# A decoder layer in float32 on one core: the small second block's high and low parts side by side in TensorE's columns, a gather's transposes moved, and the startup's weight chunks shared between two engines

## The chip, the cores and the metric

One NeuronCore of a Trainium2 chip runs the kernel. The time is the device time of one execution in microseconds (us); a kernel's time is the median of its runs. Engines are named as the profile names them: PE is TensorE (PEld its weight loads), DVE is VectorE, ACT is ScalarE, POOL is GpSimd, SP is SyncE, whose queue issues most DMAs.

## The reference

One layer of a hybrid decoder on 1024 tokens of width 1024, in float32. `c` is the conditioning vector; `w_ada` turns it into shifts, scales and gates.

```python
mod = silu(c) @ w_ada + b_ada
shift_m, scale_m, gate_m, shift_f, scale_f, gate_f = split(mod, 6)
h = rms_norm(x, norm_mix) * (1 + scale_m) + shift_m
proj = h @ w_in                                   # 1024 x 8208
...
x = x + gate_m * (sum(gates * branch_proj) @ w_out)
h = rms_norm(x, norm_ffn) * (1 + scale_f) + shift_f
y = hier_moe(h, w_group, b_group, w_router, b_router, w_gate, w_up, w_down)
x = x + gate_f * y
```

The part left out holds three causal mixers (SSD, stick-breaking attention, gated DeltaNet). `hier_moe` picks one of four groups of experts for a token and two of its eight experts; an expert e computes

```python
(silu(xi @ w_gate[e]) * (xi @ w_up[e])) @ w_down[e]      # 1024 -> 512 -> 1024
```

## The kernel before

**Products.** A float32 product is made of three in the format fp32r: each operand is split into a high part (a copy rounded to fp32r, by ACT) and a low part (the difference, by DVE or POOL), in `split` (L296). `mm3` (L301) adds high by high, high by low and low by high in one PSUM tile. The left operand is the stationary one: its columns are the output's rows, and 512 columns of the right one stream past it.

**Order.** The kernel is emitted by streams (Python generators) with priorities. `Order` (L41) keeps a clock for each engine, adds up guessed costs in `note` (L72), and `run` (L170) lets the stream go next whose data is ready, the lower priority number first; a filler stream (projections, later the experts) takes the rest of PE's time. What it decides stands fixed in each engine's instruction list; every engine works its list in order. Nearly all instructions carry line 217, that of the helper that records them, so the rows are told apart by the names of tiles.

**Startup** (`startup`, L329). Eight tiles of 128 tokens, x0 to x7 (`x_sb`, four buffers), are loaded, normed (ACT sums the squares, `rsqrt` makes twelve small DVE operations, ACT and DVE scale) and transposed by PE into `xT`; half 0 is x0 to x3, half 1 x4 to x7. In parallel `gains` computes shift and scale: w_ada's first two blocks of columns come in 16 chunks `wa` of 0.5 MB (five buffers, reloaded by `loads`), four to each of four column groups c. For c = 0 and 1 PE multiplies both halves of each chunk with c (a 1-column stationary operand, `acc_row`); for c = 2 and 3 DVE does (`acc`), and PE transposes and DVE reduces at the end. Then `modulate(half)` makes the high and low parts `hT` of the modulated tokens from `xT`, row block kt by row block kt, and `weights` splits the first columns of w_in, job 0 and 1 (`w_raw`, `w_hi`, `w_lo`; job 1 is asked for ahead of wa12). `first` (L623) makes the first six output tiles of the projections (units) from whatever row block and weights are ready, 6 times 8 times 3 products, the 48 of one more pair of tiles are made by `cols`; the next job begins with products of 264 columns.

**Experts** (`moe`, L2294, filler; `moe_tokens` and `moe_hidden`, streams). The 32 experts come in a fixed order of places; each has one block of up to 128 tokens, and the one at place 12 (`TWICE`) a second block of 64 rows (`SECOND`), unit `u = NE`. For a block, `moe_tokens` gathers token rows into `e_xg` (two buffers, an indirect DMA on POOL's queue), PE transposes them into `e_pt`, and ACT and DVE split them into `e_xh` and `e_xl`. Weights come in pieces G, U and D of two halves of 1 MB (`e_raw`); ACT and DVE split each half in two parts (`e_hi`, `e_lo`, four buffers). Gate and up products (`e_pG`, `e_pU`) are 24 each, down products (`e_pd`) 24 on the split hidden values (`e_hh`, `e_hl`), which `hidden_parts` makes; `moe_finish` scales the result by the layer's gate and adds it to the output. For the second block each weight part is used a second time at once, 72 products more, in 64 of PE's 128 columns. The second expert's transposes (n = 1 in `moe_tokens`) are asked for 4000 planner's nanoseconds after their gather.

Of the kernel before, what the change touches and what calls it, by code (L numbers as in the profile page):

```python
# [19 lines left out]
P = 128  # L20
# [20 lines left out]
class Order:  # L41
# [30 lines left out]
    def note(self, eng, method, args, kw):  # L72
# [21 lines left out]
        else:  # L94
# [7 lines left out]
            elif eng == "DVE":  # L102
                fast = method in ("tensor_scalar", "tensor_copy", "memset")
# [132 lines left out]
class Trunk:  # L236
# [92 lines left out]
    def startup(self):  # L329
# [40 lines left out]
        sums = [ps.tile([P, W], F32, name=f"acc_row{c}", tag="pj", bufs=4)[0:1] for c in range(2)]  # L370
# [31 lines left out]
        def tokens():  # L402
            for half in range(2):
                tts = range(4 * half, 4 * half + 4)
                for tt in tts:
                    yield (xs[tt],)
# [13 lines left out]
                yield tuple(xs[tt] for tt in tts)  # L420
                for kt in range(KT):
                    pt = ps.tile([P, W], F32, name=f"xT_ps{half}_{kt}", tag="ps_t", bufs=2)
                    for q in range(4):
                        self.pe.transpose(pt[:, q * P:(q + 1) * P], xs[4 * half + q][:, kt * P:(kt + 1) * P], self.ident)
                    a.activation(xT[half][:, kt], pt, AF.Copy)
                    self.done.add(f"xT{half}_{kt}")
                    yield ()
                if half == 0:
                    columns(rows[1], 32)
                    for tt in range(4, 8):  # L430
                        load_x(tt)
                    self.done.add("x_in")

        def loads():
            for n in range(5, 16):
                yield from self.wait(f"acc{n - 5}")
                if n == 12:
                    yield from self.wait("w_split0", "x_in")
                    self.job_load(1)
                load_wa()  # L440

        def gains():

            yield from self.wait("col")
            for c in range(4):
                acc = sp.tile([P, 2, 256], F32, name=f"acc{c}", tag="acc", bufs=2)
                for q in range(4):
# [13 lines left out]
                if c < 2:  # L461
                    row = acc[0:1].rearrange("p m n -> p (m n)")
                    a.activation(row, sums[c], AF.Copy)
                    yield (row,)
                    red = ps.tile([P, W], F32, name=f"acc_ps{c}", tag="ps_t", bufs=2)[:, 0:4]
                    for j in range(4):
                        self.pe.matmul(red[:, j:j + 1], row[:, j * P:(j + 1) * P], self.ones[0:1, 0:1], start=True, stop=True)
                else:
                    yield (acc,)
                    pt = ps.tile([P, W], F32, name=f"acc_ps{c}", tag="ps_t", bufs=2)  # L470
                    for j in range(4):
                        self.pe.transpose(pt[:, j * P:(j + 1) * P], acc[:, j // 2, (j % 2) * P:(j % 2 + 1) * P], self.ident)
                    red = sp.tile([P, 4], F32, name=f"red{c}", tag="red", bufs=2)
                    v.tensor_reduce(red, pt.rearrange("p (a b) -> p a b", b=P), AX.X, ALU.add)
# [6 lines left out]
        def modulate(half):  # L481
            sl = slice(half * W, (half + 1) * W)
            for kt in range(KT):
# [2146 lines left out]
```

## Time and profile before

| | us |
|---|---|
| median of 3 runs | 1964.72 |
| lowest, highest | 1963.37, 1967.28 |
| the profiled execution | 1962.96 |
| its span in the profile | 1961.2 |
| busy: PE, DVE, ACT, POOL | 1865.1, 1352.5, 1107.4, 553.0 |

The span runs from the first to the last instruction of the profiled execution. A busy time is the sum over an engine's instructions; PE and PEld overlap. The mean granted clock of PE was 0.979 of full speed. The largest groups of instructions are the splits of the experts' weights (`e_hi` 407.4 us on ACT, `e_lo` 456.5 us on DVE) and the projections' products (453.8 us for the high parts of 1408 products alone).

### The profile page before, as it was taken

To read this page: it belongs to the slowest core of one execution; us is meant where nothing else is said; L and a number is where in the kernel's file an instruction comes from. 1 tells how busy PE (TensorE), PEld (TensorE's weight loads), DVE (VectorE), ACT (ScalarE), POOL (GpSimd) and SP (SyncE) were. 2 spreads that over 40 slices of the span, in tenths; PEclk is the share of its full clock that TensorE was granted. 3 is DMA by queue.
4 is the path that set the end of the run, shared out by engine and by line. 5 is a ranking of instruction groups with operands and counts; after the bars stand their busy time and mean duration, and the time that the engine had idled before them with its cause. 6 is when DMAs were issued, how large, how long until landed. Compare 5 with 4: busy or idle time off the path is not lost. (4 is left out here: it accounts for less than half of the span.)

```text
span 1961.2 us, 29540 instructions
## 1 busy us (share of the span) xinstructions
PE 1865.1 (95%) x10069; PEld 1480.4 (75%) x10069; DVE 1352.5 (69%) x2329; ACT 1107.4 (56%) x1951; POOL 553.0 (28%) x1045
## 2 busy tenths in 40 slices
PE   5999999999999999999999998987999999999997
PEld 2797787799999988777788897875777776665553
DVE  3546776647746334666425666676999979999996
ACT  6525666632224356776534435425777857888775
POOL 2300357542426441100001034101111124444322
PEclk9999999999999999999999999987999999999999
DMA  9363666788688764432447656676999999999994
GB/s 286 81 156 102 171 181 204 217 226 226 166 193 265 179 173 119 102 92 61 87 159 218 204 166 199 237 263 239 357 350 364 364 341 329 356 324 366 378 370 128
DMA packets 331491, 441.20 MB, mean 225 GB/s; under 512 B 53686, under 2 KB 200384, under 8 KB 331338
## 3 DMA queue, kind: packets, MB, share of 16 engines
q1 hardware_dynamic: 323898, 418.80, 67.8%
q0 software_dynamic: 7296, 20.42, 4.7%
q8 instruction: 80, 1.31, 0.3%
q14 instruction: 73, 0.60, 0.1%
q10 hardware_dynamic: 144, 0.07, 0.0%
HBM read 365.15 MB, written 77.71 MB: 226 GB/s over the span
## 5 line engine op out<-in xcount | busy, mean ns | idle before, releaser
L217 ACT ACTIVATE e_hi<-e_raw 128x1024 fp32r<-128x1024 f32 (+1 forms) x386 | 407.4, 1057 | 138.0 <-PE e_pU L217 58.4
L217 DVE TENSOR_TENSOR e_lo<-e_raw,e_hi 128x1024 fp32r<-128x1024 f32 (+1 forms) x386 | 456.5, 1212 | 38.4 <-ACT e_hi L217 34.5
L217 PE MATMUL pj<-hT,w_hi 128*128 128x512 f32 x1408 | 453.8, 403 | 3.2 <-DVE m_b L217 1.3
L217 PEld LDWEIGHTS pj<-hT,w_hi 128*128 128x128 f32 x1408 | 259.5, 189 | 65.1 <-issue 8.8
L217 PE MATMUL pj<-hT,w_lo 128*128 128x512 f32 x704 | 276.6, 393 | 0.0
L217 PE MATMUL pj<-w_hi,hT 128*128 128x256 f32 (+1 forms) x1280 | 257.1, 292 | 2.1 <-ACT cv L217 0.9
L217 PEld LDWEIGHTS pj<-w_hi,hT 128*128 128x128 f32 x1280 | 207.0, 192 | 5.2 <-issue 1.7
L217 PE MATMUL pj<-w_lo,hT 128*128 128x256 f32 (+1 forms) x640 | 181.8, 284 | 0.0
L217 POOL DMA_INDIRECT out_dram<-e_y,p_row x33 | 123.9, 3756 | 182.2 <-DVE e_y L217 131.2
L217 PEld LDWEIGHTS pj<-hT,w_lo 128*128 128x128 f32 x704 | 133.0, 189 | 29.0
L217 DVE SCALAR_TENSOR_TENSOR cv<-pre,col,cv 128x512 f32<-128x512 f32 x120 | 99.7, 831 | 77.8 <-ACT cv L217 75.0
L217 DVE TENSOR_TENSOR w_lo<-w_raw,w_hi 128x512 fp32r<-128x512 f32 (+1 forms) x116 | 83.7, 721 | 96.4 <-ACT w_hi L217 93.3
L217 POOL DMA_INDIRECT e_xg<-h2D,e_idx x33 | 64.0, 1941 | 266.4 <-PE e_pt L217 242.1
L217 PEld LDWEIGHTS pj<-w_lo,hT 128*128 128x128 f32 x640 | 123.0, 192 | 0.6
L217 PE MATMUL e_pU<-e_lo,e_xh 128*128 128x512 f32 (+9 forms) x264 | 104.3, 395 | 3.7 <-DVE e_lo L217 3.7
L217 PE MATMUL e_pG<-e_hi,e_xh 128*128 128x512 f32 (+9 forms) x264 | 107.3, 406 | 0.0
L217 PE MATMUL e_pG<-e_hi,e_xl 128*128 128x512 f32 (+9 forms) x264 | 104.4, 396 | 0.0
L217 PE MATMUL e_pG<-e_lo,e_xh 128*128 128x512 f32 (+9 forms) x264 | 104.4, 395 | 0.0
L217 PE MATMUL e_pU<-e_hi,e_xh 128*128 128x512 f32 (+9 forms) x264 | 104.2, 395 | 0.0
L217 PE MATMUL e_pU<-e_hi,e_xl 128*128 128x512 f32 (+9 forms) x264 | 103.7, 393 | 0.0
L217 PE MATMUL e_pd<-e_hi,e_hh 128*128 128x512 f32 (+9 forms) x248 | 101.7, 410 | 0.0
L217 POOL TENSOR_TENSOR t_lo<-t_raw,t_hi 128x512 fp32r<-128x512 f32 x16 | 21.3, 1329 | 283.6 <-ACT t_hi L217 174.3
(470 smaller groups left out, 4006.7 us busy)
## 6 DMA issues: line engine op xcount, KB each, us to landing
e_raw<-in_w_gate_dram SPq DMA_DIRECT2D x64, 1024.0 KB
e_raw<-in_w_up_dram SPq DMA_DIRECT2D x64, 1024.0 KB
e_raw<-in_w_down_dram SPq DMA_DIRECT2D x63, 1024.0 KB
w_raw<-in_w_in_dram SPq DMA_DIRECT2D x124, 256.0 KB
m_wa<-in_w_ada_dram SPq DMA_DIRECT2D x64, 256.0 KB
brD<-br SPq DMA_DIRECT2D x48, 256.0 KB
t_raw<-in_w_branch_dram SPq DMA_DIRECT2D x16, 768.0 KB
t_gate<-brD SPq DMA_DIRECT2D x16, 768.0 KB
```

The source lines that it names most:

```text
L217: return f(*a, **k)
```

## The change

It has three parts, and one line of the planner's costs.

1. **The second block.** For unit `NE`, the high and the low part of its 64 rows lie side by side in one tile of 128 stationary columns, tokens and hidden values alike. `mm_block` makes two products where `mm3` made three: the pair with the weights' high part (output rows 0 to 63 high by high, rows 64 to 127 low by high), and the high part with the weights' low part, into rows 0 to 63. `two_parts` adds the two halves of the output: ACT copies rows 64 to 127 to rows 0 to 63 of an SBUF tile, DVE adds the others. It is used four times: gate, up, and the two halves of down.
2. **The second expert's transposes** wait for a flag "G0", set when the first expert's gate products have been emitted, in place of the 4000 ns.
3. **The startup.** Of each chunk of w_ada, PE takes one half (k = 0) and DVE the other; a column group is reduced by eight small products with a column of ones. Half 1's row blocks are modulated straight from PSUM, without the copy to `xT`, when their gain is there (`modulate(kt, half, x)`; `waiting` takes the others). x4 to x7 are loaded after wa12, job 1's weights after the last chunk; units 4 and 5 of `first` wait for the last gain; the streams have other priorities.

The planner's cost of a DVE copy or scaling is no longer the fast one where it reads PSUM.

```diff
@@ startup: tokens, loads
-                    a.activation(xT[half][:, kt], pt, AF.Copy)
-                    self.done.add(f"xT{half}_{kt}")
+                    if f"gam{kt // 2}" in self.done:
+                        modulate(kt, half, pt)
+                    else:
+                        a.activation(xT[half][:, kt], pt, AF.Copy)
+                        self.done.add(f"xT{half}_{kt}")
...
                 if half == 0:
                     columns(rows[1], 32)
-                    for tt in range(4, 8):
-                        load_x(tt)
-                    self.done.add("x_in")
+                    self.done.add("xT0")
...
-                if n == 12:
-                    yield from self.wait("w_split0", "x_in")
-                    self.job_load(1)
+                if n == 13:
+                    yield from self.wait("xT0")
+                    for tt in range(4, 8):
+                        load_x(tt)
                 load_wa()
+            yield from self.wait("w_split0")
+            self.job_load(1)
@@ startup: gains
-                    for k in range(2):
-                        kt = 2 * q + k
-                        if c < 2:
-                            self.pe.matmul(sums[c], cc[kt], was[n][:, k].rearrange("p m n -> p (m n)"), start=kt == 0, stop=kt == KT - 1)
-                        elif kt == 0:
-                            v.tensor_scalar(acc, was[n][:, k], cc[kt], None, op0=ALU.mult)
-                        else:
-                            v.scalar_tensor_tensor(acc, was[n][:, k], cc[kt], acc, op0=ALU.mult, op1=ALU.add)
+                    self.pe.matmul(sums[c % 2], cc[2 * q], was[n][:, 0].rearrange("p m n -> p (m n)"), start=q == 0, stop=q == 3)
+                    if q == 0:
+                        v.tensor_scalar(acc, was[n][:, 1], cc[1], None, op0=ALU.mult)
+                    else:
+                        v.scalar_tensor_tensor(acc, was[n][:, 1], cc[2 * q + 1], acc, op0=ALU.mult, op1=ALU.add)
...
+                for j in range(4):
+                    self.pe.matmul(red[:, j:j + 1], row[:, j * P:(j + 1) * P], self.ones[0:1, 0:1], start=True, stop=False)
+                    self.pe.matmul(red[:, j:j + 1], acc[:, j // 2, (j % 2) * P:(j % 2 + 1) * P], self.ones[:, 0:1], start=False, stop=True)
...
+            a.activation(hi, x, AF.Identity, bias=shm, scale=gam)
+            if x.space == PSUM and kt % 4 == 1:
+                a.activation(y, x, AF.Identity, bias=shm, scale=gam)
+            else:
+                v.tensor_scalar(y, x, gam, shm, op0=ALU.mult, op1=ALU.add)
+            (self.g if kt % 2 else v).tensor_tensor(lo, y, hi.bitcast(F32), ALU.subtract)
...
-        return [(0, loads()), (0, weights()), (0, gains()), (0, tokens()), (-1, modulate(0)), (-1, modulate(1))]
+        return [(0, loads()), (-1, weights()), (-2, gains()), (0, tokens()), (-1, waiting(0)), (-1, waiting(1))]
@@ first
-                u = next((u for u in range(6) if at[u] < KT and f"w{units[u][0]}_{at[u]}" in self.done
+                u = next((u for u in range(6) if at[u] < KT and (u < 4 or "gam3" in self.done) and f"w{units[u][0]}_{at[u]}" in self.done
@@ moe_tokens
-            yield [xg, 4000.0 if n == 1 else 0.0]
+            if n == 1:
+                yield from self.wait("G0")
+            yield [xg]
@@ hidden_parts
+        if e == NE:
+            self.two_parts(h, pg, n)
+            self.a.activation(sg[:n], h[:n], AF.Silu)
+            self.two_parts(h, pu, n)
+            self.v.scalar_tensor_tensor(h[:n], h[:n], w[:n], sg[:n], op0=ALU.mult, op1=ALU.mult)
...
+    def two_parts(self, out, pt, n):
+        self.a.activation(out[:n], pt[n:2 * n], AF.Copy)
+        self.v.tensor_tensor(out[:n], out[:n], pt[:n], ALU.add)
+
+    def mm_block(self, pt, x, w, u, first, last):
+        n = self.rows_of(u)
+        if u != NE:
+            self.mm3(pt[:n], x, w, first, last)
+            return
+        steps = [(pt[:2 * n], x[0], w[0]), (pt[:n], x[1], w[1])]
+        for j, (o, l, r) in enumerate(steps[::-1] if last else steps):
+            self.pe.matmul(o, l, r, start=first and j == 0, stop=last and j == 1)
```

Where the planner decides, the lists of the engines show what moved. Rows name a tile (its buffer's number behind it), what it reads, and the shape; "x2" stands for two in a row.

SP's queue in the startup, before: from the sixth chunk of w_ada (`wa`) on, with the tokens x4 to x7 (`x_sb`) and the weights of job 1 (`w_raw`).

```order
L217 DMA wa_215<-in_w_ada_dram 128x2x256 x2
L217 DMA x_sb_271<-in_x_dram 128x1024
L217 DMA x_sb_273<-in_x_dram 128x1024
L217 DMA x_sb_275<-in_x_dram 128x1024
L217 DMA x_sb_277<-in_x_dram 128x1024
L217 DMA wa_279<-in_w_ada_dram 128x2x256 x2
L217 DMA wa_291<-in_w_ada_dram 128x2x256 x2
L217 DMA wa_317<-in_w_ada_dram 128x2x256 x2
L217 DMA wa_320<-in_w_ada_dram 128x2x256 x2
L217 DMA wa_323<-in_w_ada_dram 128x2x256 x2
L217 DMA w_raw_388<-in_w_in_dram 128x2x256
```

And after the change:

```order
L217 DMA wa_313<-in_w_ada_dram 128x2x256 x2
L217 DMA wa_316<-in_w_ada_dram 128x2x256 x2
L217 DMA wa_332<-in_w_ada_dram 128x2x256 x2
L217 DMA x_sb_377<-in_x_dram 128x1024
L217 DMA x_sb_379<-in_x_dram 128x1024
L217 DMA x_sb_381<-in_x_dram 128x1024
L217 DMA x_sb_383<-in_x_dram 128x1024
L217 DMA wa_385<-in_w_ada_dram 128x2x256 x2
L217 DMA wa_388<-in_w_ada_dram 128x2x256 x2
L217 DMA wa_391<-in_w_ada_dram 128x2x256 x2
L217 DMA w_raw_394<-in_w_in_dram 128x2x256
```

x4 to x7 went out behind wa6 and now go behind wa12; job 1's weights stood ahead of wa12 and now stand behind wa15.

PE at the start of the experts, before: the transposes of the first and of the second expert's tokens (`e_xg_13987`, `e_xg_13988`) and the first gate products.

```order
L217 MATMUL e_pt_14169<-ident,e_xg_13987 128x128 x4
L217 MATMUL e_pt_14176<-ident,e_xg_13987 128x128 x4
L217 MATMUL e_pt_14189<-ident,e_xg_13988 128x128 x4
L217 MATMUL e_pG_14196<-e_hi_14131,e_xh_14167 128x512
L217 MATMUL e_pG_14196<-e_lo_14132,e_xh_14167 128x512
L217 MATMUL e_pG_14196<-e_hi_14131,e_xl_14168 128x512
```

After the change, the same place (first expert `e_xg_13997`):

```order
L217 MATMUL e_pt_14179<-ident,e_xg_13997 128x128 x4
L217 MATMUL e_pt_14186<-ident,e_xg_13997 128x128 x4
L217 MATMUL e_pG_14197<-e_hi_14141,e_xh_14177 128x512
L217 MATMUL e_pG_14197<-e_lo_14142,e_xh_14177 128x512
L217 MATMUL e_pG_14197<-e_hi_14141,e_xl_14178 128x512
```

and the end of the first expert's 24 gate products, with the second expert's transposes (`e_xg_13998`):

```order
L217 MATMUL e_pG_14197<-e_lo_14154,e_xh_14177 128x512
L217 MATMUL e_pG_14197<-e_hi_14153,e_xl_14178 128x512
L217 MATMUL e_pU_14242<-e_hi_14204,e_xh_14177 128x512
L217 MATMUL e_pU_14242<-e_lo_14205,e_xh_14177 128x512
L217 MATMUL e_pU_14242<-e_hi_14204,e_xl_14178 128x512
L217 MATMUL e_pt_14248<-ident,e_xg_13998 128x128 x4
L217 MATMUL e_pU_14242<-e_hi_14204,e_xh_14177 128x512
```

The transposes that stood ahead of the first gate product now stand behind the third up product.

PE at place 12, before: gate products of the first block (output of 128 rows) and the second (64 rows).

```order
L217 MATMUL e_pG_16591<-e_hi_16530,e_xh_16332 128x512
L217 MATMUL e_pG_16591<-e_lo_16531,e_xh_16332 128x512
L217 MATMUL e_pG_16591<-e_hi_16530,e_xl_16333 128x512
L217 MATMUL e_pG_16592<-e_hi_16530,e_xh_16514 64x512
L217 MATMUL e_pG_16592<-e_lo_16531,e_xh_16514 64x512
L217 MATMUL e_pG_16592<-e_hi_16530,e_xl_16515 64x512
L217 MATMUL e_pG_16591<-e_hi_16530,e_xh_16332 128x512
```

And after the change:

```order
L217 MATMUL e_pG_16600<-e_hi_16539,e_xh_16342 128x512
L217 MATMUL e_pG_16600<-e_lo_16540,e_xh_16342 128x512
L217 MATMUL e_pG_16600<-e_hi_16539,e_xl_16343 128x512
L217 MATMUL e_pG_16601<-e_hi_16539,e_xh_16524 128x512
L217 MATMUL e_pG_16601<-e_lo_16540,e_xh_16524 64x512
L217 MATMUL e_pG_16600<-e_hi_16539,e_xh_16342 128x512
```

The second block's three products have become two, of 128 and of 64 output rows.

## Rows read from the trace of the kernel before

**Rows 1.** Page, part 1: busy us of each engine (share of the span), instructions.

```profile
PE 1865.1 (95%) x10069; PEld 1480.4 (75%) x10069; DVE 1352.5 (69%) x2329; ACT 1107.4 (56%) x1951; POOL 553.0 (28%) x1045
```

**Rows 2.** Timeline of PE, startup: start us, us, engine, line, operation, tiles, shape, count.

```profile
20.99 1.15 PE L217 MATMUL xT_ps<-ident,x_sb 128*128 128x128 f32 x8 [0.25 <-ACT xT L217]
...
57.22 1.20 PE L217 MATMUL pj<-hT,w_hi 128*128 128x512 f32 x2
...
59.92 1.05 PE L217 MATMUL pj<-hT,w_hi 128*128 128x512 f32 x2
...
63.22 0.62 PE L217 MATMUL pj<-hT,w_hi 128*128 128x512 f32 x2
...
63.90 0.62 PE L217 MATMUL pj<-hT,w_hi 128*128 128x512 f32 x2
...
102.58 0.28 PE L217 MATMUL pj<-w_hi,hT 128*128 128x264 f32 x1
```

**Rows 3.** Windows of the startup: stretch, its length, busy us by engine, PEclk, DMA share, GB/s.

```profile
0.00:44.00 44.00, 27.00 (x95) 10.46 (x95) 10.71 (x38) 25.63 (x44) 8.26 (x18) 1.00 0.95 285
...
44.00:52.00 8.00, 5.08 (x24) 3.50 (x23) 7.86 (x10) 7.25 (x13) 3.66 (x3) 0.79 0.94 278
...
52.00:60.00 8.00, 5.32 (x19) 4.11 (x20) 6.48 (x11) 6.85 (x14) 5.29 (x6) 0.64 0.31 44
...
64.00:100.00 36.00, 34.54 (x153) 27.86 (x152) 16.81 (x25) 14.40 (x28) 11.63 (x12) 1.00 0.33 82
```

**Rows 4.** Timeline of DVE, startup.

```profile
38.83 0.70 DVE L217 TENSOR_SCALAR rs_x<-rs_x 128x4 f32<-128x4 f32 x1
...
42.22 0.16 DVE L217 TENSOR_TENSOR rs_t<-rs_t,rs_x 128x4 f32<-128x4 f32 x1
...
43.35 2.33 DVE L217 SCALAR_TENSOR_TENSOR acc<-wa,col,acc 128x512 f32<-128x512 f32 x3
...
45.59 1.41 DVE L217 TENSOR_SCALAR x_sb<-x_sb,x_rstd 128x1024 f32<-128x1024 f32 x2
...
46.91 2.43 DVE L217 SCALAR_TENSOR_TENSOR acc<-wa,col,acc 128x512 f32<-128x512 f32 x2
```

**Rows 5.** Timeline of SP's queue, startup (DMA issues).

```profile
24.53 1.89 SPq L217 DMA_DIRECT2D x_sb<-in_x_dram  x4
```

**Rows 6.** Window of the recurrences, columns as in rows 3.

```profile
564.00:608.00 44.00, 42.66 (x344) 40.72 (x344) 25.76 (x53) 13.96 (x41) 16.03 (x63) 1.00 0.79 238
```

**Rows 7.** Timeline of PE, start of the experts.

```profile
1330.55 1.94 PE L217 MATMUL e_pt<-ident,e_xg 128*128 128x128 f32 x8 [5.51 <-DMA e_xg<-h2D,e_idx]
...
1339.78 1.09 PE L217 MATMUL e_pt<-ident,e_xg 128*128 128x128 f32 x4 [7.29 <-DMA e_xg<-h2D,e_idx]
...
1340.52 0.78 PE L217 MATMUL e_pG<-e_hi,e_xh 128*128 128x512 f32 x1
```

**Rows 8.** Timeline of ACT, start of the experts.

```profile
1331.72 0.60 ACT L217 ACTIVATE e_xh<-e_pt 128x512 fp32r<-128x512 f32 x1 [6.47 <-PE e_pt L217]
```

**Rows 9.** Timeline of DVE, start of the experts.

```profile
1332.35 1.50 DVE L217 TENSOR_TENSOR e_xl<-e_pt,e_xh 128x512 fp32r<-128x512 f32 x2 [2.58 <-ACT e_xh L217]
```

**Rows 10.** Windows among the experts, columns as in rows 3.

```profile
1380.00:1440.00 60.00, 56.11 (x281) 44.02 (x280) 59.62 (x103) 44.18 (x49) 13.75 (x7) 1.00 1.03 359
...
1560.00:1600.00 40.00, 40.00 (x191) 28.35 (x190) 28.25 (x31) 23.81 (x29) 4.71 (x3) 1.00 1.01 347
```

**Rows 11.** Timeline of PE, gate products of the two blocks at place 12.

```profile
1568.67 0.40 PE L217 MATMUL e_pG<-e_hi,e_xh 128*64 128x512 f32 x1
...
1568.91 0.39 PE L217 MATMUL e_pG<-e_lo,e_xh 128*64 128x512 f32 x1
```

**Rows 12.** Waits of PE, 1500 to 1930 us: waiter, releaser, us in total, times, longest.

```profile
PE e_pU L217 <- DVE e_lo L217: 0.4, 1, 0.4
```

**Rows 13.** Timeline of DVE, second block.

```profile
1574.78 1.22 DVE L217 TENSOR_TENSOR e_lo<-e_raw,e_hi 128x1024 fp32r<-128x1024 f32 x1 [1.52 <-ACT e_hi L217]
...
1624.29 0.68 DVE L217 TENSOR_TENSOR e_y<-e_pG,gate_f 64x512 f32<-64x512 f32 x1
```

More of the change, by code (lines that the diff above doesn't have):

```diff
@@ L102, in note @@
             elif eng == "DVE":
-                fast = method in ("tensor_scalar", "tensor_copy", "memset")
+                fast = method in ("tensor_scalar", "tensor_copy", "memset") and not (ins and ins[0].space == PSUM)
                 c = (0.52 if fast else 1.042) * big + 68 + 61 * min(percol, 1)
@@ L369, in startup @@
         cc = [col[:, kt:kt + 1] for kt in range(KT)]
-        sums = [ps.tile([P, W], F32, name=f"acc_row{c}", tag="pj", bufs=4)[0:1] for c in range(2)]
+        sums = [ps.tile([P, W], F32, name=f"acc_row{j}", tag="pj", bufs=4)[0:1] for j in range(2)]
         load_x(0)
@@ L405, in tokens @@
                 for tt in tts:
+                    while len(xs) <= tt:
+                        yield BLOCKED
                     yield (xs[tt],)
@@ new lines, in gains @@
+                    if q == 0:
+                        v.tensor_scalar(acc, was[n][:, 1], cc[1], None, op0=ALU.mult)
+                    else:
+                        v.scalar_tensor_tensor(acc, was[n][:, 1], cc[2 * q + 1], acc, op0=ALU.mult, op1=ALU.add)
+                    self.done.add(f"acc{n}")
+                row = sp.tile([1, W], F32, name=f"row{c}", tag="row", bufs=2)
+                a.activation(row, sums[c % 2], AF.Copy)
+                yield (row, acc)
+                red = ps.tile([P, W], F32, name=f"acc_ps{c}", tag="ps_t", bufs=2)[:, 0:4]
@@ L479, in gains, with modulate, waiting @@
                 self.done.add(f"gam{c}")
-        def modulate(half):
+        def modulate(kt, half, x):
             sl = slice(half * W, (half + 1) * W)
-            for kt in range(KT):
-                yield from self.wait(f"gam{kt // 2}", f"xT{half}_{kt}")
-                x = xT[half][:, kt]
-                yield (x, self.gam[:, kt:kt + 1])
-                a.activation(self.hT[0][:, kt, sl], x, AF.Identity, bias=self.shm[:, kt:kt + 1], scale=self.gam[:, kt:kt + 1])
-                if kt % 2:
-                    a.activation(x, x, AF.Identity, bias=self.shm[:, kt:kt + 1], scale=self.gam[:, kt:kt + 1])
-                else:
-                    v.tensor_scalar(x, x, self.gam[:, kt:kt + 1], self.shm[:, kt:kt + 1], op0=ALU.mult, op1=ALU.add)
-                (self.g if kt % 2 else v).tensor_tensor(self.hT[1][:, kt, sl], x, self.hT[0][:, kt, sl].bitcast(F32), ALU.subtract)
-                self.done.add(f"h{half}_{kt}")
+            hi, lo = self.hT[0][:, kt, sl], self.hT[1][:, kt, sl]
+            gam, shm = self.gam[:, kt:kt + 1], self.shm[:, kt:kt + 1]
+            y = xT[half][:, kt]
+            a.activation(hi, x, AF.Identity, bias=shm, scale=gam)
[4 more added lines that the diff above has]
+            (self.g if kt % 2 else v).tensor_tensor(lo, y, hi.bitcast(F32), ALU.subtract)
+            self.done.add(f"h{half}_{kt}")
+        def waiting(half):
+            for kt in range(KT):
+                yield from self.wait(f"gam{kt // 2}")
+                while not {f"xT{half}_{kt}", f"h{half}_{kt}"} & self.done:
+                    yield BLOCKED
+                if f"h{half}_{kt}" not in self.done:
+                    x = xT[half][:, kt]
+                    yield (x, self.gam[:, kt:kt + 1])
+                    modulate(kt, half, x)
         def weights():
@@ L2239, in token_parts @@
         hi = self.ep.tile([P, KT, P], F32R, name=self.nm("e_xh"), tag="e_xh", bufs=2)
-        lo = self.ep.tile([P, KT, P], F32R, name=self.nm("e_xl"), tag="e_xl", bufs=2)
-        self.order.track(W, hi, lo)
+        if e == NE:
+            both, lo = hi, hi[:, :, n:2 * n]
+            self.order.track(W, hi)
+        else:
+            lo = self.ep.tile([P, KT, P], F32R, name=self.nm("e_xl"), tag="e_xl", bufs=2)
+            self.order.track(W, hi, lo)
         for h in range(2):
@@ L2247, in token_parts @@
             yield
[L2248 removed]
+        self.xT[e] = (both[:, :, 0:2 * n], both[:, :, 0:n]) if e == NE else (hi[:, :, :n], lo[:, :, :n])
         self.done.add(f"x{e}")
@@ L2384, in moe @@
                         xT = self.xT[u]
-                        self.mm3(self.pgu[u][-1][:self.rows_of(u)], (xT[0][:, kk], xT[1][:, kk]), w, kk == 0, kk == KT - 1)
+                        self.mm_block(self.pgu[u][-1], (xT[0][:, kk], xT[1][:, kk]), w, u, kk == 0, kk == KT - 1)
                     ahead(n, q)
                     yield
-                if kind == "U" and kh == 1:
-                    self.done.add(f"U{e}")
+                if kh == 1:
+                    self.done.add(f"{kind}{e}")
     NB = 32
```

41 lines of the change are left out of this document (19 added, 22 removed).

## The prediction

> **What bounds the kernel now.** I read the page's busy times first: TensorE (PE) works 95% of the span, VectorE (DVE) 69% [rows 1]. So the time is PE's work plus the few stretches in which it has none, and each part of the change is priced there. The windows and PE's timeline name three such places.
>
> Startup: PE has little to do until its unbroken products begin at 57.22 us. After that they run to the first product of the next projection job at 102.58 us, the last point that stands alike in both orders [rows 2]. A window shows the loads at 285 GB/s until 44 us, then almost no loading from 52 to 60 us, and a granted clock of 0.79 and 0.64 in the idle stretch, 1.00 afterwards [rows 3].
>
> Start of the experts: PE transposes the first expert's tokens at 1330.55 us, then waits 7.29 us for the second expert's gather before the first product at 1340.52 us [rows 7].
>
> The experts themselves: from 1500 to 1930 us PE waits once, 0.4 us [rows 12]; in 1560 to 1600 us, where the second block lies, it is busy 40.00 of 40 us [rows 10]. A product taken out there is time.
>
> **Second block.** 72 products become 48: each of 24 steps loses one. A 64-column product takes the same pitch as a 128-column one; two in a row start 0.24 us apart [rows 11], 0.227 over a longer run (three products from 63.22 to 63.90 us, at full clock [rows 2]). 24 × 0.227 = **5.4 us** off PE. The wider of the two products left costs no more, since the pitch goes by the 512 moving columns. Added: four ScalarE (ACT) copies and four DVE additions of 64x512. An operation of that size takes DVE 0.68 us [rows 13], so 4 × 0.68 = 2.7 us on DVE and, by the same row, at most about as much on ACT. I cost both at nothing: in 1560 to 1600 us DVE is busy 28.25 and ACT 23.81 of 40 us [rows 10], and DVE idles 1.52 us before an e_lo [rows 13]. Queued behind the added operations are the next expert's e_hi and e_lo, which PE uses four parts later. If that cover is gone, the 2.7 us come back. Bounds: 2.7 and 5.5 us.
>
> **Start of the experts.** The second expert's eight transposes move behind the first expert's 24 gate products, into its up products. What the first product then waits for is e_xh: ACT writes its first half at 1331.72 + 0.60 = 1332.3 us [rows 8], and PE's own transposes end at 1330.55 + 1.94 = 1332.5 us [rows 7]. The third product needs e_xl's first half, about 0.7 us into DVE's pair that starts at 1332.35 us [rows 9], so 1333.1 us, and is not due before 1333.4 at half clock. So the first product starts near 1332.6 instead of 1340.52, 7.9 us earlier. The first four transposes, which now take the 0.74 us ahead of that product [rows 7], return later for about 0.5: **7.4 us**. If the first product waits for the whole of e_xl (1332.35 + 1.50 and a hand-over), it starts at 1334.1, and 5.9 us are left; the upper bound is 8. The gather comes well before its new place, at 1339.8 against the 24 products' end near 1341. GpSimd (POOL)'s queue has a later gather that waits for the same transposes: they now end around 1344, as they did (about 1345), so it is not late. Behind that place DVE is the full engine, 59.62 of 60 us from 1380 to 1440, with PE at 56.11 [rows 10]; its work starts earlier by the same amount, so I let the gain stand.
>
> **Startup.** Both kernels run the same 16 fp32 products and 16 DVE passes over w_ada's 16 chunks; what changes is when. Each chunk is read by PE and DVE together, so a column group's gain is ready soon after its chunks, and half 0 gets six of its eight row blocks (36 products) before half 1 starts, where 12 were done. In exchange x4 to x7 move behind wa12 on SP's queue (they went out at 24.53 us [rows 5]).
> - Loads: up to wa14 there are x (4 MB), 15 chunks of 0.5 MB, 1 MB of w_in and the small rows, 12.6 MB; at 285 GB/s [rows 3] that is 44.2 us.
> - Then, in DVE's order, one pass over wa14, the twelve small operations of the norm, one pass over wa15, two scalings of x. Alone that is 0.8 + 12 × 0.2 + 0.8 + 1.4 = 5.4 us; beside POOL, where small operations took up to 0.70 instead of 0.16 and a pass 1.22 instead of 0.78 [rows 4], 1.2 + 4.7 + 1.2 + 1.4 = 8.5 us (4.7 by the third to the eleventh of the twelve: nine from 38.83 to 42.38 us, 0.39 each [rows 4]). I take 6.5, nearer the free price, since before this POOL worked beside only a part of them: half 1 starts at **50.7 us** (49.6 to 52.7).
> - PE then has 192 − 36 = 156 products, 35.4 us, 32 transposes at 1.15/8 us [rows 2], 4.6 us, and an overhead. Before, 180 products (40.8 us) took 102.58 − 57.22 = 45.4 us, so 4.6 of half clock and waits; with more work at hand I take 3 (1.5 to 6).
> - 50.7 + 35.4 + 4.6 + 3 = 93.7 us against 102.58: **8.9 us**. With the ends, 91.1 to 98.7 us: 3.9 to 11.5 us gained.
>
> The eight ACT copies and the reductions that go lay in the stretch where PE waited, and are in that sum. Here a rule weighs against the change. The rows show DVE operations stretched fourfold while POOL subtracts [rows 4]. The Trainium skill, "SBUF — State Buffer", section "Who interferes with whom", says that a DVE instruction with two SBUF inputs and a GpSimd instruction that reads SBUF contend, one blocking the other for its whole length. By it all of half 1's low parts would go in single file on the two engines, and the startup would gain some 2 us less; the rows show stretches, not always, so I keep the sum.
>
> Between 564 and 608 us the order of the recurrences' small steps also changes, among the same products. PE is busy 42.66 of 44 us there [rows 6]: 1.3 us to win, a few hops to lose (+3); I take 0.
>
> **Sum.** 8.9 + 7.4 + 5.4 = 21.7 us. The profiled execution took 1962.96 us (span 1961.2), so 1941.3; the median shown is 1964.72, 1.8 above it, so **1943.0 us**. A measurement here tells about 0.2%, 3.9 us, from no change.
>
> **Rivals.**
> - A. Half 1's low parts come late: DVE and POOL hand one another the way, PE waits per row block, and its 48 products of half 1 made in that stretch go at half clock, as those at 57.22 to 59.92 us did (2.70 us for 6, 0.45 each [rows 2]). 48 × 0.223 = 10.7 us: 1953.7. For it: rows 4 and the clock of 0.64 [rows 3]. Against: half 1 asks 13 operations of 512 columns of DVE, 8.8 us at the 0.68 of [rows 13], for 48 × 0.227 + 4.6 = 15.5 us of PE. The page named above would give this as its extreme case.
> - E. SP's queue stands still once more, as from 52 to 60 us, when 44 GB/s moved [rows 3]: 8 × (1 − 44/285) = 6.8 us of loading, now ahead of x4 to x7: 1949.8. Each reload waits for both readers of the chunk five before.
> - B. The gain at the experts' start is lost behind it, DVE being full [rows 10]: 1950.4.
> - C. The second block gives nothing, since the weights come no faster or the additions are in the way: 1948.4. Against: the weights stay ahead of PE [rows 12].
> - D, slower. The clock stays at the lower level (1.2 GHz) through the whole first projection, because PE never gets unbroken work after the scattered products of half 0. 156 × 0.223 = 34.8 us: 1977.8. It decides from (21.7 + 3.9)/0.223 = 115 products on. Against: in 64 to 100 us the clock was 1.00, after a like start [rows 3].
> - F. The change doesn't do what it says, or two of A, B, C, E together with a late load cancel it: 1964.7.
>
> **How the numbers follow.** Forecast 0.62, A 0.11, B 0.08, E 0.06, C 0.05, D 0.04, F 0.04. The forecast's own range is 1939 to 1952: from the lower bounds 3.9 + 5.9 + 2.7 = 12.5 to the upper 11.5 + 8 + 5.5 = 25. Taking in A, B, C and E it is 1937 to 1955, which leaves out D, F and the mishaps that pile up. Faster: all but D and F, 0.92; same: F, 0.04; slower: D, 0.04.
>
> **What the profile after would show.** Right: half 1's first transposes near 51 us, the first gate-width product of the next job near 94 us at clock 1.00; the first e_pG product right behind eight transposes near 1332.6 − 8.9 = 1323.7 us, with no wait for a gather; in the second block starts of 64- and 128-column products still 0.23 us apart, two a step, and PE without idle time. Wrong: DVE or POOL as releaser of pj products for several us; a hole in the loads ahead of x4 to x7; the granted clock below 1.00 after 70 us; or PE waiting for e_lo or e_xl more than the 0.4 us of [rows 12].

## The result and the profile after

The changed kernel takes 1951.65 us (median of 4 runs, 1947.1 to 1951.8), the kernel before 1966.0 in the same comparison (4 runs, 1963.37 to 1968.42): ratio 0.9919, 95% interval 0.9903 to 0.9935, so 15.9 us less (12.8 to 19.1); the medians lie 14.35 us apart, the profiled executions, 1962.96 and 1947.10, 15.86. Forecast were 21.7 us less. The time lies in the range and the direction is right, but 6 us of the expected gain are missing, and they are what the experiments look for.

The page's busy times after, which answer to [rows 1]:

```profile
PE 1865.7 (96%) x10085; PEld 1481.8 (76%) x10085; DVE 1353.4 (70%) x2337; ACT 1100.9 (57%) x1943; POOL 544.7 (28%) x1045
```

PE is busy as long as before, 1865.1 us; what went is idle time (the span was 1961.2, now 1945.0).

To see where the time came from, the table takes four points that both kernels pass with the same instruction, in each profiled execution: the first product of 264 columns, the first transposes of the experts' start, the first gate product at place 12, and that of place 16, behind the second block. The lead is before's start less the other's; every number is a row of a PE timeline or a difference of two.

| kernel | 264 columns | experts' start | place 12 | place 16 | lead at these |
|---|---|---|---|---|---|
| before | 102.58 | 1330.55 | 1567.89 | 1656.36 | |
| changed | 94.87 | 1319.88 | 1551.62 | 1639.67 | 7.7, 10.7, 16.3, 16.7 |
| changed, second profile | 97.35 | 1327.36 | 1558.21 | 1646.25 | 5.2, 3.2, 9.7, 10.1 |
| e1 (without part 2) | 95.30 | 1322.29 | 1560.35 | 1648.48 | 7.3, 8.3, 7.5, 7.9 |
| e2 (without part 1) | 96.70 | 1324.98 | 1556.26 | 1644.56 | 5.9, 5.6, 11.6, 11.8 |
| e3 (without part 3) | 102.49 | 1333.24 | 1564.02 | 1652.08 | 0.1, −2.7, 3.9, 4.3 |
| e4 (gate sum early) | 96.83 | 1324.26 | 1556.08 | 1644.94 | 5.8, 6.3, 11.8, 11.4 |
| e5 (o_p later) | 97.59 | 1328.50 | 1562.14 | 1650.06 | 5.0, 2.1, 5.8, 6.3 |
| e7 (sums spread) | 97.84 | 1327.69 | 1558.55 | 1642.41 | 4.7, 2.9, 9.3, 14.0 |
| e8 (e5 and e7) | 99.42 | 1326.34 | 1560.41 | 1644.27 | 3.2, 4.2, 7.5, 12.1 |
| e9 (x4 to x7 after wa9) | 105.45 | 1333.55 | 1564.82 | 1654.40 | −2.9, −3.0, 3.1, 2.0 |
| e10 (reduction folded) | 97.58 | 1322.28 | 1553.13 | 1641.18 | 5.0, 8.3, 14.8, 15.2 |
| e11 (e7 and e10) | 97.53 | 1324.23 | 1556.30 | 1640.14 | 5.1, 6.3, 11.6, 16.2 |

Two things are seen at once. Between the first two points, where no product went, single executions win or lose up to 3.3 us without a pattern. From place 12 to 16 the change wins 0.4 us instead of 5.4, in both of its profiles, and so do e1, e3 and e10, which leave the second block as it is (0.3 to 0.4).

**Startup.** PE's timeline after, against [rows 2]:

```profile
51.57 0.38 PE L217 MATMUL acc_ps<-ones,row 1*128 1x1 f32 x2
...
53.74 0.38 PE L217 MATMUL acc_ps<-ones,acc 128*128 128x1 f32 x2
53.98 1.18 PE L217 MATMUL xT_ps<-ident,x_sb 128*128 128x128 f32 x8
...
94.87 0.28 PE L217 MATMUL pj<-w_hi,hT 128*128 128x264 f32 x1
```

Half 1's transposes start at 53.98 us, behind eight small one-column products, two instructions each, that turn the last gain into columns (51.57 to 53.98).

**Experts' start.** PE's timeline after, against [rows 7]:

```profile
1319.88 1.94 PE L217 MATMUL e_pt<-ident,e_xg 128*128 128x128 f32 x8 [5.72 <-DMA e_xg<-h2D,e_idx]
1321.75 0.76 PE L217 MATMUL e_pG<-e_hi,e_xh 128*128 128x512 f32 x1
...
1323.17 0.46 PE L217 MATMUL e_pG<-e_hi,e_xh 128*128 128x512 f32 x1
...
1352.67 0.24 PE L217 MATMUL o_p<-o_t,ones 32*32 32x32 f32 x2 [2.14 <-DVE e_xl L217]
1353.46 0.66 PE L217 MATMUL e_pt<-ident,e_xg 128*128 128x128 f32 x4 [0.55 <-DVE p_c L217]
...
1354.32 0.63 PE L217 MATMUL e_pd<-e_lo,e_hh 128*128 128x512 f32 x1
```

The first gate product follows the transposes without a wait, at half clock for three products only. Some 30 us later PE waits 2.14 us for e_xl and 0.55 for p_c, and the products after that run at 0.43 us a piece: the second stop gives back part of what the first one won. PE doesn't wait for a value there: o_p reads `o_t`, which DVE had written at 1348.28 us. By the kernel's text o_p and all transposes of the experts share two PSUM buffers (tag `tp`), and one comes free only when DVE's e_xl has read the transposes in it; that e_xl (1351.94 us) stands behind three e_lo.

**Second block.** PE, then ACT and DVE, behind the gate products of place 13:

```profile
1587.85 0.47 PE L217 MATMUL e_pU<-e_hi,e_xh 128*96 128x512 f32 x1 [0.62 <-ACT e_hi L217]
1589.48 0.72 PE L217 MATMUL e_pU<-e_lo,e_xh 128*96 128x512 f32 x1 [1.16 <-DVE e_lo L217]
...
1591.71 0.63 PE L217 MATMUL e_pU<-e_lo,e_xh 128*96 128x512 f32 x1
1592.13 0.63 PE L217 MATMUL e_pU<-e_hi,e_xl 128*96 128x512 f32 x1
...
1610.66 0.46 PE L217 MATMUL e_pU<-e_lo,e_xh 128*88 128x512 f32 x1 [1.79 <-DVE e_lo L217]
```

```profile
1582.51 0.60 ACT L217 ACTIVATE e_h<-e_pG 64x512 f32<-64x512 f32 x1
1585.11 0.63 ACT L217 ACTIVATE e_sg<-e_h 64x512 f32<-64x512 f32 x1 [2.00 <-DVE e_h L217]
1585.77 0.59 ACT L217 ACTIVATE e_h<-e_pU 64x512 f32<-64x512 f32 x1
...
1586.75 3.89 ACT L217 ACTIVATE e_hi<-e_raw 128x1024 fp32r<-128x1024 f32 x4
```

```profile
1581.00 3.48 DVE L217 TENSOR_TENSOR e_lo<-e_raw,e_hi 128x1024 fp32r<-128x1024 f32 x3
1584.40 0.67 DVE L217 TENSOR_TENSOR e_h<-e_h,e_pG 64x512 f32<-64x512 f32 x1
1586.40 0.68 DVE L217 TENSOR_TENSOR e_h<-e_h,e_pU 64x512 f32<-64x512 f32 x1 [1.33 <-ACT e_h L217]
...
1588.21 4.61 DVE L217 TENSOR_TENSOR e_lo<-e_raw,e_hi 128x1024 fp32r<-128x1024 f32 x4
...
1606.30 0.67 DVE L217 TENSOR_TENSOR e_y<-e_y,e_pG 64x512 f32<-64x512 f32 x1
...
1608.32 0.68 DVE L217 TENSOR_TENSOR e_y<-e_y,gate_f 64x512 f32<-64x512 f32 x1
...
1609.40 9.15 DVE L217 TENSOR_TENSOR e_lo<-e_raw,e_hi 128x1024 fp32r<-128x1024 f32 x8
```

ACT copies the low half (1582.51), then holds its queue for 2.00 us, since silu (1585.11) wants DVE's sum, which stands behind three e_lo (1581.00, 3.48 us). The next four e_hi come only at 1586.75 and their e_lo at 1588.21; PE waits 0.62 and 1.16 us, and the products behind run at half clock (0.42 apart at 1591.71). The up products of place 13 take 9.64 us (to 1592.56) where they took 6.10. At 1610.66 PE waits once more, behind the four DVE operations of the second block's output (1606.30 to 1608.32, two before the change).

The half clock is not what costs here. In the second profile the same two waits (0.62 and 1.15 us) were followed by products at full clock, and PE then waited for the low part of the second block's hidden values, which stands in DVE's queue behind four e_lo; the gain from place 12 to 16 was the same 0.4 us:

```profile
1599.81 0.50 PE L217 MATMUL e_pG<-e_hi,e_hh 128*128 128x512 f32 x1 [1.09 <-DVE e_hh L217]
```

### The profile page after: what moved, and what is told of

Same layout as the page of the kernel before. It is cut to its first block, busy times and chain, and to the rows that moved or that the text cites. A ratio compares the mean times of both kernels' runs of the same rounds, so it can differ in the third digit from the quotient of the medians.

```text
span 1945.0 us, 29567 instructions
## 1 busy us (share of the span) xinstructions
PE 1865.7 (96%) x10085; PEld 1481.8 (76%) x10085; DVE 1353.4 (70%) x2337; ACT 1100.9 (57%) x1943; POOL 544.7 (28%) x1045
## 5 line engine op out<-in xcount | busy, mean ns | idle before, releaser
L217 POOL DMA_INDIRECT e_xg<-h2D,e_idx x33 | 58.9, 1785 | 280.9 <-PE e_pt L217 234.5
```

Source lines behind the costliest of these rows:

```text
L217: return f(*a, **k)
```

## The experiments

All ratios are to the kernel before, run beside each kernel on the same chip. The changed kernel's two medians lie 3 us apart, so steps are read from the traces, and the times are given beside them. Theory S is the reading of the first profile given above; the rivals' letters are those of each expectation.

**a0. The changed kernel again.** No edit.

> The changed kernel itself, as a yardstick for the other kernels of this call: 13 us faster than before (11 to 16), since the profiled execution that the comparison was read from was its fastest. Its trace: first product of 264 columns at 95 to 99 us, later where the granted clock falls to half behind the small one-column products of the reductions.

1948.61 us against 1966.06, ratio 0.9911 (0.9893 to 0.9929): 17.5 us less. Its profiled execution, 1953.49, was its slowest, as the first comparison's was the fastest. The change is thus worth 14 to 17.5 us by the medians, and a single profile can stand 5 us off its kernel's median. The one profile of before, 1962.96, is 3.0 below before's median of 1966.0, and every lead in the table is taken against it.

**e1. Without part 2.**

```diff
-            if n == 1:
-                yield from self.wait("G0")
-            yield [xg]
+            yield [xg, 4000.0 if n == 1 else 0.0]
```

> The changed kernel without its second part: the second expert's transposes are asked for 4000 planner's ns after their gather again, ahead of the first gate products. Theory S (steps of the trace): the profile's steps give this part 8.1 us at the first product and take 4.6 us back where the small products o_p wait for VectorE's e_xl, net 5.6 us, so this kernel should be 5.6 us slower than the changed one (4 to 7). Rival V: VectorE is the full engine from there to about 1500 us, so its total work sets the end and the part is worth nothing, 0 us (-1 to 1). Rival F, the forecast's own term: 7.4 us.

1960.23 us, ratio 0.9976 (0.9961 to 0.9992). From the experts' start to place 12 it loses 0.7 us against before where the changed kernel wins 5.6 (second profile 6.5): the part is worth 6 to 7 us there, a little over theory S, and rival V falls. By its time e1 is some 11 us behind the changed kernel (the ratios differ by 0.0057; an estimate from the two intervals is 7 to 16 us), more than the step and both theories give; where the rest arises is not shown, and the profile is of the fastest of its eight executions. Its PE stands as before the change did:

```profile
1331.29 1.09 PE L217 MATMUL e_pt<-ident,e_xg 128*128 128x128 f32 x4 [7.07 <-DMA e_xg<-h2D,e_idx]
1332.03 0.78 PE L217 MATMUL e_pG<-e_hi,e_xh 128*128 128x512 f32 x1
```

**e2. Without part 1.** `mm_block` and `two_parts` are taken out again; the second block uses `mm3`.

```diff
-                        self.mm_block(self.pgu[u][-1], (xT[0][:, kk], xT[1][:, kk]), w, u, kk == 0, kk == KT - 1)
+                        self.mm3(self.pgu[u][-1][:self.rows_of(u)], (xT[0][:, kk], xT[1][:, kk]), w, kk == 0, kk == KT - 1)
```

> The changed kernel without its first part: the second block is computed with three products and without the halves' sums. Theory S: of 5.3 us of products saved, 3.5 us go where ScalarE's queue stands before the first sums (waits of 1.8 us and the lower clock after them) and 1.3 us at the output's sums, so the part is worth 0.4 us: this kernel should be within 1 us of the changed one. Rival F, the forecast's term: 5.4 us slower. Rival W: without the sums PE runs on and the weights come too late anyway, then also about 0, but with waits for e_lo or e_hi in the trace where theory S has none.

1951.86 us, ratio 0.9926 (0.9905 to 0.9947). From place 12 to 16 its lead grows by 0.2 us, the changed kernel's by 0.4: the part as it stands is worth nothing. PE's waits from 1550 to 1640 us, of e2 and of the changed kernel, columns as in [rows 12]:

```profile
PE e_pU L217 <- DVE e_lo L217: 0.2, 1, 0.2
```

```profile
PE e_pU L217 <- DVE e_lo L217: 2.9, 2, 1.8
PE e_pU L217 <- ACT e_hi L217: 0.6, 1, 0.6
```

Without the sums PE doesn't wait there. So the waits come with the sums. That alone doesn't rule rival W out, since e2's PE also takes its 24 more products to get there; e7, with the short list of products and little waiting, does.

**e3. Without part 3.** The hunks of `startup` and `first` are taken back; the planner's new cost stays.

> The changed kernel without its third part: startup as before (the planner's new cost for VectorE kept). Theory S: 7.7 us slower than the changed one (6.5 to 9), all of it before the first product of 264 columns, and the order of the recurrences' steps unchanged against the changed kernel. Rival G: the lead of the startup is partly waited away in the recurrences, where loads and chains through DRAM set the pace, 3 to 5 us. Forecast's term: 8.9 us.

1961.08 us, ratio 0.9981 (0.9969 to 0.9993). The first product of 264 columns is at 102.49 us as before, against 94.87 to 99.42 in the eight profiles with the new startup (median 97.1): the part is worth about 5.5 us there. The other steps stay: 6.6 us at the experts' start, 0.4 at the second block. By its time e3 is some 12 us behind the changed kernel (0.0062 in the ratios, 8 to 16 us by the same estimate), over theory S and the forecast's term, and not rival G's 3 to 5. Between the first two points its profile lost 2.8 us more; what else makes up the difference is not shown.

**e4. The gate's sum early, the output's product on GpSimd.**

```diff
+    def second_gate(self):
+        yield from self.wait(f"G{self.TWICE}")
...
+        self.two_parts(g, self.pgu[NE][0], n)
+        yield [g]
+        self.a.activation(g[:n], g[:n], AF.Silu)
...
-            self.v.tensor_tensor(y[:n, cs], (y[:, cs] if e == NE else pd[nb])[:n], self.gate_f[:n, cs], ALU.mult)
+            (self.g if e == NE else self.v).tensor_tensor(y[:n, cs], (y[:, cs] if e == NE else pd[nb])[:n], self.gate_f[:n, cs], ALU.mult)
```

> The changed kernel with the second block's sums moved: the gate's two halves are summed and put through silu while the up products run (a stream of its own that lets other work between the copy, the sum and the silu), and the output's product with the gate goes to GpSimd. Theory S: the stalls of 3.5 and 1.3 us behind the second block shrink to about 1 us in all, so 3.5 us faster than the changed kernel (2 to 5). Rival W: the weights are what comes too late there, 0 us, with PE waiting for ACT or DVE that wait for a load.

1955.05 us, ratio 0.9943 (0.9923 to 0.9963); expected were 2 to 5 us less than the changed kernel. The first stall went: the lead is 15.3 us before and after the up products of place 13. Then it shrank to 11.4 over two waits, the first for the hidden low part behind DVE's three e_lo, as in the second profile of the changed kernel. DVE, POOL and PE there:

```profile
1609.85 0.54 DVE L217 TENSOR_TENSOR e_hl<-e_ph,e_hh 128x384 fp32r<-128x384 f32 x1
1610.31 8.46 DVE L217 TENSOR_TENSOR e_lo<-e_raw,e_hi 128x1024 fp32r<-128x1024 f32 x5
```

```profile
1610.08 3.06 POOL L217 TENSOR_TENSOR e_y<-e_y,gate_f 64x512 f32<-64x512 f32 x2
```

```profile
1595.68 0.50 PE L217 MATMUL e_pG<-e_hi,e_hh 128*128 128x512 f32 x1 [1.34 <-DVE e_hh L217]
...
1614.28 0.46 PE L217 MATMUL e_pU<-e_lo,e_xh 128*88 128x512 f32 x1 [3.07 <-DVE e_lo L217]
```

While POOL multiplied two SBUF operands for 3.06 us, five e_lo took 8.46 us, where eight took 9.15 without it in the changed kernel (1609.40 above), 1.14 each: 2.7 us too many. PE waited 3.07 us, 1.28 more than in the changed kernel, and its products ran at half clock behind it. Half of theory S was confirmed, and the cure for the other half made a stall of its own.

**e5. The small products later.**

```diff
         v.tensor_copy(tabT, tab)
-        yield 1000.0
+        yield 4000.0
```

> The changed kernel with the small products o_p of the second table of experts asked for 4000 planner's ns after their inputs, not 1000. Theory S: in the changed kernel PE stands 2.1 us before o_p and 0.5 before the next transposes, and its clock falls for the following ten products (1.6 us); with o_p later these 4 us come back: 3 us faster than the changed one (2 to 4.5), the lead over the kernel before at the third expert's gate products about as large as at the first's. Rival V: VectorE is the full engine there and the same wait comes back at e_lo or e_xl: 0 us (-1 to 1).

1957.23 us, ratio 0.9948 (0.9931 to 0.9965). Theory S falls here: from the first gate product to place 12 the lead shrinks by 4.4 us (10.2 to 5.8), in the changed kernel by 2.5.

```profile
1362.54 0.24 PE L217 MATMUL o_p<-o_t,ones 32*32 32x32 f32 x2
...
1366.31 0.66 PE L217 MATMUL e_ph<-ident,e_h 128*128 128x128 f32 x4 [1.93 <-DVE e_xl L217]
...
1368.23 0.63 PE L217 MATMUL e_pG<-e_lo,e_xh 128*128 128x512 f32 x1
...
1373.12 0.63 PE L217 MATMUL e_pG<-e_hi,e_xh 128*128 128x512 f32 x1
```

```profile
1362.17 3.47 DVE L217 TENSOR_TENSOR e_lo<-e_raw,e_hi 128x1024 fp32r<-128x1024 f32 x3
1365.58 0.67 DVE L217 TENSOR_TENSOR e_xl<-e_pt,e_xh 128x512 fp32r<-128x512 f32 x1
```

o_p itself no longer waits, but the transposes behind it wait 1.93 us for the next e_xl, which again stands behind three e_lo, and products then run at half clock until 1373.5. It was not o_p's place: DVE is behind there, as rival V had it, and whatever needs one of the two PSUM buffers next waits. A third buffer was not tried.

**e7. All sums in streams of their own, on ACT and DVE.**

```diff
+    def second_sums(self):
...
+        self.two_parts(g, self.pgu[NE][0], n)
+        yield [g]
+        self.a.activation(g[:n], g[:n], AF.Silu)
+        yield from self.wait(f"U{self.TWICE}")
+        self.two_parts(h, self.pgu[NE][1], n)
+        yield [h]
...
+    def second_out(self):
...
+            yield 1500.0
+            self.two_parts(y[:, cs], pd[nb], n)
+            yield 1500.0
+            self.v.tensor_tensor(y[:n, cs], y[:n, cs], self.gate_f[:n, cs], ALU.mult)
```

> The changed kernel with all sums of the second block in streams of their own: the gate's sum and silu under the up products, the up sum right behind them, the output's sums and gate products 1500 planner's ns apart, all on ScalarE and VectorE (none on GpSimd). Theory S: no PE wait over 0.7 us from the gate products at place 12 to the end, the lead over the kernel before grows there by 5 us (4 to 5.5) and stays: 4 us faster than the changed kernel (3 to 5). Rival X: VectorE has no room for the two additions more, wherever they stand; then a wait for e_lo of 1 us or more stays and the gain is 2 us or less. Rival W: the weights come too late there: 0 us.

1949.58 us, ratio 0.9919 (0.9901 to 0.9936). From place 12 to 16 the lead grows by 4.6 us (9.3 to 14.0) and stays. PE's waits from 1550 to 1660 us:

```profile
PE e_pU L217 <- DVE e_lo L217: 0.8, 1, 0.8
PE e_pt L217 <- DVE e_xl L217: 0.3, 1, 0.3
```

The same products, the same sums, 4.2 us more: it was where the sums stood in the two queues. Rival X falls, with no wait of 1 us left, and rival W: the weights were in time. By its time the kernel isn't told apart from the changed one (expected were 4 us less); in this profile its startup and recurrences were 8 us slower (2.9 us of lead at the experts' start against 10.7). By their medians, the same edit gave 8.2 us on top of e5 (e8) and 2.4 on top of e10 (e11).

**e8. e5 and e7 together.**

> e5 and e7 together. Theory S: their gains add up, as PE is the bound from there on: 7 us faster than the changed kernel (5 to 9). Rival B: the loads of the weights cannot follow, and PE, ACT or VectorE wait for e_raw in the second half: 4 us or less.

1949.04 us, ratio 0.9911 (0.9894 to 0.9928). Behind place 12 the lead grows by 4.6 us as in e7; ahead of it 4.8 are lost as in e5. They add up, with e5's sign the wrong one; the 7 us expected against the changed kernel did not come.

**e9. x4 to x7 behind wa9.**

```diff
-                if n == 13:
+                if n == 10:
                     yield from self.wait("xT0")
```

> The changed kernel with x4 to x7 loaded behind wa9 instead of wa12. Theory S: half 1's transposes started at 54.0 us, 3.3 later than forecast, since the norm's small operations stood behind VectorE's pass over wa14 (which landed near 46.5) and PE's eight reductions ahead of the transposes; with x earlier the norm comes ahead of the last chunks, the last gain comes as late as before, and half 0 loses what half 1 gains: the first product of 264 columns within 1 us of the changed kernel's. Rival T: half 1's start alone sets the end: 2 us earlier (1.5 to 3).

1956.76 us, ratio 0.9949 (0.9932 to 0.9965), and both theories miss: the first product of 264 columns is at 105.45 us. Half 1's transposes (53.94 us) now stand ahead of the last gain's small products. By the kernel's text both use the same two PSUM buffers (tag `ps_t`), and PE waits 2.85 us until DVE has read a transposed block out of one (at 57.83 us). The granted clock is 0.50 from 48 to 52 and from 60 to 66 us.

```profile
53.94 1.09 PE L217 MATMUL xT_ps<-ident,x_sb 128*128 128x128 f32 x8
57.88 0.38 PE L217 MATMUL acc_ps<-ones,row 1*128 1x1 f32 x2 [2.85 <-DVE xT L217]
```

**e10 and e11. The reduction folded**, alone and together with e7.

```diff
+                self.pe.matmul(sums[c % 2], self.ones[:, 0:1], acc.rearrange("p m n -> p (m n)"), start=False, stop=True)
...
-                    self.pe.matmul(red[:, j:j + 1], acc[:, j // 2, (j % 2) * P:(j % 2 + 1) * P], self.ones[:, 0:1], start=False, stop=True)
```

> The changed kernel with VectorE's partial sums added into PE's row by one product with a column of ones per column group, so that four small products per group turn the row into columns where there were eight. Theory C: a group's eight small products cost PE 2.5 us and, in most profiled executions, some 3 us of half clock behind them (0.50 at 44 to 46 us or at 56 to 60 us while PE is busy all the time); with half as many in a row both shrink: 3 us faster than the changed kernel (1 to 5), first product of 264 columns at 92 to 95 us and the clock at 1.00 from 36 to 64 us. Rival D: the clock does not go by these products; then only the difference of the products counts, 4 times 0.3 us less, and the added step in the chain of the last gain takes about as much: 0 us (-1 to 1).

> Both: the reduction folded and the second block's sums in streams of their own. Theory C and S: 7 us faster than the changed kernel (5 to 9), as the two places lie apart and PE is the bound behind each. Rival: if the startup's lead is waited away before the experts, 4 us, from the sums alone.

e10: 1950.09 us, ratio 0.9925 (0.9906 to 0.9943); e11: 1947.68 us, 0.9908 (0.9889 to 0.9927). Windows of e10 and of a0, columns as in [rows 3]:

```profile
36.00:44.00 8.00, 8.00 (x28) 3.17 (x27) 4.72 (x12) 4.19 (x7) 1.29 (x1) 1.00 1.05 385
...
52.00:60.00 8.00, 6.53 (x32) 4.58 (x31) 3.60 (x8) 5.29 (x9) 2.73 (x3) 0.87 0.01 1
```

```profile
36.00:44.00 8.00, 8.00 (x31) 4.53 (x30) 4.01 (x10) 5.99 (x11) 1.28 (x1) 0.91 1.05 386
...
52.00:60.00 8.00, 8.00 (x40) 6.86 (x40) 2.29 (x6) 6.26 (x10) 2.63 (x4) 0.79 0.27 26
```

With fewer small products the clock is 1.00 up to 52 us, as theory C has it, but PE is idle for 1.5 us in the next window (a wait for DVE's reading of a PSUM buffer, as in e9), the clock falls then, and the 264-column product comes at 97.58 against 97.35: rival D's sum, though not its reason. e11 keeps the 4.6 us of the second block and has the lowest median of all kernels here, but it is 0.9 us under a0, where its theory had 7 and its rival 4, and its interval covers the changed kernel's.

## Why the prediction was right, and where it was not

The direction and the three places were right. The measured 1951.65 us lies 8.6 us above the forecast of 1943.0, only 0.35 us inside the forecast's own range, and nearer to the times of rivals A and B than to the forecast's. That it lies in the range is owed to wide bounds and, in the first profile, to 3 us of luck (below). One of the signs of being wrong that the prediction named came true: from 1500 to 1930 us PE waited 2.9 us for e_lo where it had waited 0.4, and at 1352 us 2.14 for e_xl.

**Second block: the saving right, the cost wrong.** Forecast 5.4 us, measured 0.4. The lead grew by 3.55 us over the gate and up products and by 1.7 over the down products, 5.3 in all, as 24 × 0.227 said. The step that failed is "I cost both at nothing", with the cover read from windows of 20 and 40 us and from idle time before one e_lo. The sums aren't spread over that window; they are a chain with four hand-overs between ACT's and DVE's queues, and the e_hi and e_lo that PE needs next stood behind it. The prediction saw them there, but took the four parts that PE has in hand as cover enough. The lower bound of 2.7 us priced DVE's work, not the queues' standing still. This was rival C, by its "additions in the way"; its other half, late weights, was ruled out by e7.

**Experts' start: right.** The first product came 1.87 us after the transposes' start (forecast 2.05) and won 8.1 us (7.9). Of the part's 7.4 us, 6 to 7 remained by the step (e1). What is missing is rival B in small: DVE was late for e_xl at 1352 us.

**Startup: the gain smaller, by terms that partly cancelled.** Forecast 8.9 us, measured at the first 264-column product 7.7 in the first profile and 5.5 by the median of eight. Half 1 started at 54.0, not 50.7: DVE was done with wa14 at 47.65 us, about 2.5 later than forecast, the last tile of x was scaled by ACT at 52.8, and the small products of the reduction, which the sum didn't price on PE, stood ahead of the transposes until 54.0. The overhead was 0.9 us instead of 3 (54.0 + 35.4 + 4.6 = 94.0). In six of the other seven profiles PE was busy and yet at half clock for some 3 us at one or two places. Rival A did not come: PE waited for a low part 0.29 us. E did not either, and D's clock only in short pieces. The time of e3 would give the part more than the forecast, not less; that contradiction is open.

**Between 564 and 608 us** nothing was forecast; e3, with the same order of PE's products there, lost 2.8 us from the first 264-column product to the experts' start, where the changed kernel won 3.0 and its second profile lost 2.0. So it is scatter, and the first profile's 3 us were luck.

**The sum.** In the first profile the steps add up to the 16.2 us by which the span is shorter: 7.7, 3.0, 5.6, 0.4, and −0.5 behind place 16. Against the forecast 1.2, 1.8, 5.0 and 0.5 are missing, and the lucky 3.0 are there in their place. With the steps that several profiles show (5.5, 6 to 7, 0.4) the three parts come to some 12.5 us, where the medians say 14 to 17.5; that before's profile was 3.0 us under its median may explain this. The times without one part (11, 1 and 12 us) add up to more than the change is worth, so how the gain divides between parts 2 and 3 is known to some 5 us only. That part 1 gave nothing doesn't hang on this.

## What to carry to other kernels

A saved product on the bounding engine is worth its time only if what replaces it finds a place in the other engines' queues; ask what stands behind each added operation, not how busy the engine is on average. A chain that crosses two in-order queues should be emitted in pieces, with room for the work behind it, and its first piece as early as its data is there (e7: 4.2 us from order alone). When PE waits for an operation whose result it doesn't read, look for a buffer that the operation frees. When single profiles scatter by some us, compare leads at points both kernels pass, in more than one profile of each.

## What the runs showed of the hardware

A wait of PE can cost more than itself: after 1.93 us of idle time in e5 the granted clock was at its lower level (1.2 GHz) for some 13 products, 0.43 us apart instead of 0.23; in the first profile of the changed kernel the waits at 1352 us were followed by eight such products. It need not: in the second profile the same waits, 2.13 and 0.55 us, were followed by products 0.23 us apart.

```profile
1360.80 0.24 PE L217 MATMUL o_p<-o_t,ones 32*32 32x32 f32 x2 [2.13 <-DVE e_xl L217]
...
1362.33 0.39 PE L217 MATMUL e_pd<-e_lo,e_hh 128*128 128x512 f32 x1
1362.56 0.39 PE L217 MATMUL e_pd<-e_hi,e_hl 128*128 128x512 f32 x1
```

The clock also fell with PE busy throughout. In e7, behind a row of small one-column products:

```profile
40.00:42.00 2.00, 2.00 (x14) 1.91 (x14) 1.40 (x3) 1.52 (x3) 0.49 (x1) 1.00 1.00 388
42.00:44.00 2.00, 2.00 (x6) 0.78 (x7) 0.78 (x4) 1.86 (x3) 0.77 (x1) 0.73 1.08 352
44.00:46.00 2.00, 2.00 (x6) 1.54 (x6) 0.79 (x2) 2.00 (x5) 0.00 (x0) 0.50 1.09 348
46.00:48.00 2.00, 2.00 (x9) 1.27 (x8) 1.97 (x4) 0.89 (x2) 1.01 (x1) 0.92 1.12 268
```

In the first profile of the changed kernel, with the same order, it stayed at 1.00 through this stretch; what decides between the two is left open. It explains most of the startup's scatter: of the eight profiles with the new startup the clock stayed at 1.00 from 40 to 70 us in two, with the 264-column product at 94.87 and 95.30 us, and fell in the other six, with that product at 96.70 to 99.42.

The stretched e_lo beside POOL's product in e4 show one engine held up by the other, for 2.7 us of POOL's 3.06. The Trainium skill, "SBUF — State Buffer", section "Who interferes with whom", says that a DVE instruction with two SBUF inputs contends with a GpSimd instruction that reads SBUF, and the trace agrees. In the startup of the changed kernel two DVE passes over w_ada took 2.44 us beside a subtraction of POOL (at 45.28 us) and 1.54 without one (at 35.61). For half 1's low parts, where the prediction weighed that rule, PE waited 0.29 us in all; it had other row blocks to work on.
